# The mixer's input projection by Strassen products, with kept weight sums and equal buffers

## The chip, the cores and the metric

The kernel runs on one core of a Trainium2 chip. The metric is the time of one execution on the device in microseconds. The engines are TensorE (PE: matmuls and transposes; its weight loads, PEld, overlap them), VectorE (DVE), ScalarE (ACT), GpSimd (POOL) and SyncE (SP), on whose queue all DMAs of this kernel are issued. Each engine works through its own instructions in a fixed order and waits on semaphores for the others. SBUF is the memory on the core, PSUM the memory that matmuls write, DRAM lies outside.

## What is computed

One layer of a decoder, for a prompt of 2048 tokens and 32 sample tokens (8 sequences of 4), with a model width of 1024, all in float32. Cut to what matters here:

```python
def token_mixer(xn, mem_k, mem_v, pool_prev, n_prev, lp):       # xn = rmsnorm(x)
    proj = xn @ lp['w_in']                  # 1024 x 4608: u 512 | v 512 | pool 256 | queries 256 | gates 3 x 1024
    u, v = jnp.split(jax.nn.gelu(a_part), 2, axis=-1)
    vn = layernorm(v, lp['gmlp_ln_g'], lp['gmlp_ln_b'])
    br_a = (u * chunk_spatial(vn, ...)) @ lp['w_branch_a']
    br_b = mixed_pools(b_part) @ lp['w_branch_b']               # causal means over 2, 4, 8, 16 tokens
    br_c = cross_attn(q, mem_k, mem_v) @ lp['w_branch_c']       # 4 heads of 64, softmax over 256 memory tokens
    merged = gates[0] * br_a + gates[1] * br_b + gates[2] * br_c
    return merged @ lp['w_out'], vn, new_pool

def decoder_layer(...):
    h = x + rmsnorm(token_mixer(rmsnorm(x), ...))
    out = h + rmsnorm(conv_ffn(rmsnorm(h), ...))                # 1024 -> 2 x 2816 -> 1024
```

## The kernel before

Products that need float32 accuracy are made of three matmuls. Both factors are split into a rounded part (hi) and the rest (lo), and hi x hi, hi x lo and lo x hi are added up in PSUM. `split_unit` (L104) splits a weight tile: ScalarE casts (L109), VectorE subtracts (L110); its results lie in a ring of three buffers, `u`. Weights come into SBUF through the pool `rawp`, two buffers of 8 KB per partition.

The prompt is worked through in four blocks of 512 tokens, 0 to 3; block 1 has the 32 sample tokens too, 544 in all, as two column ranges of 272. For each block `mixer` runs over the columns of `w_in`: the v stage (tokens in rows, `tok_mm`, L129 to L131), then sixteen pairs of 128-column tiles (`mtile`, L124 to L126: 8 steps of depth, three matmuls each, so 24 of 512 columns a tile and 48 a pair): one pair for the pool, one for the queries, two for u and twelve for the gates. Each tile's result is evicted by one ScalarE instruction (L657 for u with its gelu, L695 for a gate with its tanh). After each three gate pairs the three branches' matrices follow for two column tiles (again `mtile`), and VectorE multiplies and adds (L708 to L714).

Between queries and u stands the cross-attention, for four row tiles of 128 tokens: scores (L613), maximum (L619), exponentials (L622), reciprocal and scaling (L624, L626), transposes (L632), their copies to SBUF (L635, one by ScalarE and one by VectorE), the product with the values (L641), and the split of its result (L645, L646). The tiles `pr` (probabilities) and `pT` (transposed) come from the pool `w4` of four buffers of 4 KB, which many short-lived tiles share.

`outproj` multiplies the merged result by `w_out`, normalises and adds x. Beside it, `norm_steps` prepares the next block's x: normalisation (L164), transposes (L174), split (L178, L179). In blocks 2 and 3 `pair_steps` prepares the FFN's x beside the gates: it fetches rows of h from DRAM, scales them (L264), transposes (L275, L277), forms the sums of quarters that Strassen's products need and stores them in DRAM.

The FFN's first matrix is already multiplied by seven Strassen products instead of eight (L873): `right_factors` (L309) forms sums of the weights' quarters (L320 to L324), `blocks` multiplies and combines.

The order of the instructions on each engine is set when the program is built: a scheduler of the framework places each instruction by priority (program order) and by when it takes its operands and buffers to be free. The generators (`next(steps)`) only set where in program order a step stands.

## Time and profile before

| | |
|---|---|
| median of 3 runs | 2811.24 us (2808.88 to 2812.51) |
| the profiled execution | 2814.71 us, span of its instructions 2813.0 us |
| TensorE busy | 2752.8 us, 98% |
| VectorE, ScalarE busy | 1710.2 us (61%), 1037.3 us (37%) |
| mean granted TensorE clock | 0.991 |
| DMA | 337.57 MB, mean 120 GB/s |

The stages in the span: up to 136 us the start, v, pool, queries, attention and u of block 0; to 314 us its gates; to 363 its output projection; block 1 to 760 us with its gates from 504 on; block 2 to 1058; block 3 to 1373; the two halves of the FFN's first matrix to 1845 and 2291; the second matrix to the end. A matmul's end is modelled in these records and successive matmuls overlap; what one costs is the distance between two starts. The granted clock is the share of TensorE's full clock that the chip let through.

### The profile page before, as it was taken

What the parts mean: (1) busy time and instruction counts of PE and PEld (TensorE: products, weight loads), DVE (VectorE), ACT (ScalarE), POOL (GpSimd) and SP (SyncE); (2) the same over time, 40 slices, a digit from 0 to 9 for tenths busy, and PEclk for the clock granted to TensorE, in tenths of its full rate; (3) what the DMA queues carried; (4) which work ended last, traced back from release to release, by engine and by line L of the source; (5) the groups of instructions that cost most, each with busy time, mean ns of one, the idle gap of its engine ahead of it and who ended that gap; (6) DMA issues with size and microseconds to landing.
All of it is one profiled execution on the core that took longest, in us unless ns stands there. A gap on an engine that the chain in (4) does not pass through costs nothing.

```text
span 2813.0 us, 38162 instructions
## 1 busy us (share of the span) xinstructions
PE 2752.8 (98%) x15256; PEld 2361.8 (84%) x15256; DVE 1710.2 (61%) x2777; ACT 1037.3 (37%) x1676; POOL 108.0 (4%) x192
## 2 busy tenths in 40 slices
PE   7999999999999999999999999989999989999998
PEld 6688889999778887888788888889999978888887
DVE  5534465343464546544587877667777756668665
ACT  3532334333554435443554543332332332214112
POOL 1000010000100001000100000000000000001001
PEclk9999999999999999999999999999999999999999
DMA  5323333322325433355553432522122243225322
GB/s 178 113 90 97 125 121 102 102 91 91 125 86 157 155 120 120 113 165 190 206 169 102 141 123 80 204 101 92 61 77 92 69 165 131 90 78 205 109 73 92
DMA packets 256916, 337.57 MB, mean 120 GB/s; under 512 B 16365, under 2 KB 211194, under 8 KB 254938
## 3 DMA queue, kind: packets, MB, share of 16 engines
q1 hardware_dynamic: 256738, 335.13, 35.8%
q8 instruction: 120, 1.97, 0.3%
q14 instruction: 58, 0.48, 0.1%
HBM read 270.22 MB, written 64.96 MB: 119 GB/s over the span
## 4 chain that ended last, share of the span: by engine, by line
issue 52%; PE 42%; DVE 2%; POOL 2%; ACT 1%; DMA 0%; POOLq 0%; SPq 0%; DVEq 0%; ACTq 0%
PE mm L126 10%; PE mm L125 10%; PE mm L124 10%; PE mm L129 2%; PE mm L131 2%; PE mm L130 2%; POOL rs L136 1%; POOL rs L138 1%; PE tp L613 1%; PE tp L641 1%; ACT tp L151 1%; PE mm L439 1%; PE tp L660 1%; PE tp L632 0%; PE tp L174 0%
## 5 line engine op out<-in xcount | busy, mean ns | idle before, releaser
L873 PE MATMUL mm<-X,u 128*128 128x512 f32 (+2 forms) x5544 | 896.5, 323 | 13.4 <-ACT u L109 4.1
L873 PEld LDWEIGHTS mm<-X,u 128*128 128x128 f32 x5544 | 802.9, 190 | 98.5 <-ACT u L109 6.7
L110 DVE TENSOR_TENSOR u<-raw,u 128x1024 fp32r<-128x1024 f32 (+1 forms) x384 | 445.1, 1160 | 514.0 <-ACT u L109 513.7
L109 ACT CAST u<-raw 128x1024 fp32r<-128x1024 f32 (+1 forms) x384 | 382.5, 1000 | 711.4 <-PE mm L131 235.6
L126 PE MATMUL mm<-half,u 128*128 128x512 f32 (+1 forms) x1600 | 566.8, 354 | 4.4 <-DVE u L110 4.4
L124 PE MATMUL mm<-half,u 128*128 128x512 f32 (+1 forms) x1600 | 567.2, 354 | 0.0
L125 PE MATMUL mm<-half,u 128*128 128x512 f32 (+1 forms) x1600 | 566.3, 354 | 0.0
L126 PEld LDWEIGHTS mm<-half,u 128*128 128x128 f32 x1600 | 301.5, 188 | 47.4 <-DVE u L110 5.7
L124 PEld LDWEIGHTS mm<-half,u 128*128 128x128 f32 x1600 | 301.9, 189 | 43.5 <-issue 0.3
L125 PEld LDWEIGHTS mm<-half,u 128*128 128x128 f32 x1600 | 301.7, 189 | 42.3
L1036 DVE TENSOR_TENSOR Y<-Y,mm 128x512 f32<-128x512 f32 (+1 forms) x340 | 212.0, 636 | 135.1 <-PE mm L131 126.4
L129 PE MATMUL mm<-u,a 128*128 128x512 f32 x616 | 242.6, 394 | 7.3 <-ACT a L1023 7.3
L131 PE MATMUL mm<-u,a 128*128 128x512 f32 x616 | 245.6, 399 | 0.4 <-DVE a L1024 0.4
L130 PE MATMUL mm<-u,a 128*128 128x512 f32 x616 | 244.7, 397 | 0.0
L695 ACT ACTIVATE gt<-mm,vb 128x512 f32<-128x512 f32 (+1 forms) x120 | 73.0, 609 | 337.8 <-PE mm L126 337.8
L129 PE MATMUL mm<-u,half 128*128 128x512 f32 (+1 forms) x360 | 145.1, 403 | 2.3 <-ACT half L178 2.3
L129 PEld LDWEIGHTS mm<-u,a 128*128 128x128 f32 x616 | 117.7, 191 | 34.2 <-ACT a L1023 7.5
L131 PE MATMUL mm<-u,half 128*128 128x512 f32 (+1 forms) x360 | 143.0, 398 | 0.0
L130 PE MATMUL mm<-u,half 128*128 128x512 f32 (+1 forms) x360 | 142.6, 396 | 0.0
L130 PEld LDWEIGHTS mm<-u,a 128*128 128x128 f32 x616 | 116.4, 189 | 27.3
L131 PEld LDWEIGHTS mm<-u,a 128*128 128x128 f32 x616 | 116.3, 189 | 27.0 <-DVE a L1024 1.1
L956 DVE SCALAR_TENSOR_TENSOR d<-gE,vecs,d 128x1024 f32<-128x1024 f32 x88 | 112.7, 1280 | 1.2 <-ACT d L954 0.2
(237 smaller groups left out, 2692.7 us busy)
## 6 DMA issues: line engine op xcount, KB each, us to landing
raw<-in_w_in SPq DMA_DIRECT2D x72, 1024.0 KB
raw<-in_w_up SPq DMA_DIRECT2D x44, 1024.0 KB
raw<-in_w_down SPq DMA_DIRECT2D x22, 1024.0 KB
raw<-in_w_out SPq DMA_DIRECT2D x16, 1024.0 KB
act<-d SPq DMA_DIRECT2D x22, 528.0 KB
ar<-act SPq DMA_DIRECT2D x22, 528.0 KB
act<-d SPq DMA_DIRECT2D x22, 512.0 KB
ar<-act SPq DMA_DIRECT2D x22, 512.0 KB
```

Source lines behind the costliest of these rows:

```text
L109: S.copy(uv[:, 0], src)
L110: V.tensor_tensor(uv[:, 1], src, uv[:, 0].bitcast(F32), ALU.subtract)
L124: T.matmul(ps, lhsT=u[:, 0, k], rhs=xk(xT, k, 0, c0, n), start=i == 0, stop=False)
L125: T.matmul(ps, lhsT=u[:, 0, k], rhs=xk(xT, k, 1, c0, n), start=False, stop=False)
L126: T.matmul(ps, lhsT=u[:, 1, k], rhs=xk(xT, k, 0, c0, n), start=False, stop=i == len(ks) - 1)
L129: T.matmul(ps, lhsT=lh, rhs=wh, start=first, stop=False)
L130: T.matmul(ps, lhsT=lh, rhs=wl, start=False, stop=False)
L131: T.matmul(ps, lhsT=ll, rhs=wh, start=False, stop=last)
L695: S.activation(gt[:, c0:c0 + n], ps[:, :n], AF.Tanh, bias=vb[:, i * 8 + j:i * 8 + j + 1], scale=0.5)
L873: T.matmul(ps, lhsT=u[:, wl, k], rhs=x[:, xl, k, c0:c0 + n], start=not more and k + i == 0, stop=k + i == 5, skip_group_check=True)
L956: V.scalar_tensor_tensor(d[j][:, 0:FSB], gE[j][:, k:k + FSB], cw(k, f), d[j][:, 0:FSB], ALU.mult, ALU.add)
L1036: return V.tensor_tensor(yd, yd, ps, ALU.add)
```

## The change

- All sixteen pairs of `w_in` in every block are computed by `blocks`, with the block's tokens in two halves of 256 rows (272 in block 1), the depth in two halves of 512 and the pair's two column tiles as the two halves of the columns: 7 products of 12 matmuls with 256 (272) columns.
- The seven combinations of x are made by `mix_steps` and `pair_steps` in the gate stage of the block before, stored in DRAM (`md`, `m8`, `mf_`) and loaded by `load_block` in the output projection; block 0 makes its own at the start. `norm_steps` and `to_features` are gone.
- The sums of the weights are formed in block 0 by `right_factors` and stored in DRAM (`ws`); blocks 1 to 3 load them by `kept_factors`, 1.75 MB a pair, split as 3.5 tiles of 128x1024.
- A pair's results leave PSUM by one copy (p1) and four instructions of 256 columns on ScalarE and five of 256 columns on VectorE.
- In the v stage the sample rows of block 1 are two parts of 16 rows. The attention over the samples' cached memory now stands directly behind the prompt's attention.
- Buffers: `big`, 6 of 17 KB, becomes 13 of 8.5 KB; `rawp` becomes 4 of 4 KB, `w2` 8 instead of 10; weights and down weights are loaded in smaller pieces. The tile t1 of a pair (p1, v, v7 and one more) is one buffer of `w4`; in the mixer the weight sums `sm` too.

```diff
-    big = ctx.enter_context(tc.tile_pool(name="big", bufs=6))
-    rawp = ctx.enter_context(tc.tile_pool(name="rawp", bufs=2))
+    big = ctx.enter_context(tc.tile_pool(name="big", bufs=13))
+    rawp = ctx.enter_context(tc.tile_pool(name="rawp", bufs=4))
...
+    def mix_steps(b):
+
+        for r1, r2, n, _ in mix_rows(b):
+            for src, i in (r1, r2):
+                xt = w4.tile([P, D], F32, name="xt", tag="w4")
+                DMA.dma_start(xt[:n], src)
+                row_rstd(xt[:n], n, rx[:n, i:i + 1])
+            yield
...
+        yield from pair_steps(items, gx)
...
+    def kept_factors(c):
+
+        return factors_of(split_unit(raw3(load_raw(w_in[:, :, c:c + P]), 8)),
+                          split_unit(raw3(load_raw(ws[c][:, 0:8]), 8)),
+                          split_unit(raw3(load_raw(ws[c][:, 12:16]), 8)[:, 0:4]),
+                          split_unit(raw3(load_raw(ws[c][:, 8:12], w_in[:, 4:8, c + P:c + 2 * P]), 8)))
...
+    def blocks(W, X, c0, n):
+
+
+        if n <= 256:
+            t1 = w4.tile([P, D], F32, name="t1", tag="w4")
+            p1, v, v7, sp = (t1[:, q * 256:q * 256 + n] for q in range(4))
...
+        pa = mm()[:, :n]
+        product(pa, W[1], factor(X, 1), c0, n)
+        S.copy(p1, pa)
+        yield
+        pb = mm()[:, :n]
+        product(pb, W[6], factor(X, 6), c0, n)
+        V.tensor_tensor(v, pb, p1, ALU.subtract)
+        yield
+        product(pa, W[2], factor(X, 2), c0, n, True)
+        yield 0, 0, pa, None, None, sp
+        pc = mm()[:, :n]
+        product(pc, W[7], factor(X, 7), c0, n)
+        V.tensor_tensor(v7, pc, v, ALU.add)
+        yield
+        pe = mm()[:, :n]
+        product(pe, W[4], factor(X, 4), c0, n)
+        yield 1, 0, pe, v7, ALU.subtract, sp
+        pd = mm()[:, :n]
+        product(pd, W[5], factor(X, 5), c0, n)
+        yield 1, 1, pd, v7, ALU.add, sp
+        product(pd, W[3], factor(X, 3), c0, n, True)
+        yield 0, 1, pd, v, ALU.add, sp
...
+            def pair(c):
+                W = kept_factors(c) if b else right_factors(w_in, c)
+                for _, _, (h, *it) in all_blocks(W, X, [(0, w)], False):
+                    yield (h, *it)
...
             for gp in range(2):
-                pu = pair_units(w_in[:, :, gp * 256:gp * 256 + 256])
+                ugs = [w2.tile([P, NTB], F32, name="ug", tag="w2") for _ in range(2)]
+                for h, j, *it in pair(gp * 256):
+                    spread(ugs[j], whole(h, j, *it), h, lambda o, i: S.activation(o, i, AF.Gelu_apprx_tanh))
...
-                    for jj in range(2):
-                        j = 2 * jp + jj
-                        u = pu(jj)
-                        gt = w2.tile([P, NTB], F32, name="gt", tag="w2")
-                        for (c0, n) in subs:
-                            ps = mm()
-                            mtile(ps[:, :n], u, xT, c0, n)
-                            S.activation(gt[:, c0:c0 + n], ps[:, :n], AF.Tanh,
-                                         bias=vb[:, i * 8 + j:i * 8 + j + 1], scale=0.5)
+                    for _ in range(3 if b == 2 else 2):
+                        next(steps, None)
+                    gt = [w2.tile([P, NTB], F32, name="gt", tag="w2") for _ in range(2)]
+                    for h, j, *it in pair(1536 + i * D + jp * 256):
+                        r = i * 8 + 2 * jp + j
+                        spread(gt[j], whole(h, j, *it), h,
+                               lambda o, x: S.activation(o, x, AF.Tanh, bias=vb[:, r:r + 1], scale=0.5))
```

The order of instructions around two places. TensorE in the attention of block 2, before: scores L613, transposes L632, values L641; L124 to L126 are matmuls of the u stage. The excerpt goes from the third row tile's transposes to the fourth's scores.

```order
L126 MATMUL mm<-half,u 128x512
L632 MATMUL tp<-ident,pr 128x128 x6
L124 MATMUL mm<-half,u 128x512
L632 MATMUL tp<-ident,pr 128x128 x2
L641 MATMUL tp<-pT,Vm 64x128 x4
L613 MATMUL tp<-kT,qq 128x256 x4
L641 MATMUL tp<-pT,Vm 64x128 x4
L613 MATMUL tp<-kT,qq 128x256 x8
L125 MATMUL mm<-half,u 128x512
L126 MATMUL mm<-half,u 128x512
L124 MATMUL mm<-half,u 128x512
```

Fifteen matmuls of the u stage stand behind these scores, ahead of the fourth tile's transposes, and about as many ahead of the third's. The same place in the changed kernel, from the second row tile's scores to the third's transposes (scores L719, transposes L738, values L747; L381 are products of the u pair):

```order
L719 MATMUL tp<-kT,qq 128x256 x10
L381 MATMUL mm<-xs,u 128x256 x10
L738 MATMUL tp<-ident,pr 128x128 x8
L747 MATMUL tp<-pT,Vm 64x128 x4
L719 MATMUL tp<-kT,qq 128x256 x2
L747 MATMUL tp<-pT,Vm 64x128 x4
L719 MATMUL tp<-kT,qq 128x256 x10
L738 MATMUL tp<-ident,pr 128x128 x8
```

Ten matmuls of 256 columns stand ahead of the second tile's transposes and none ahead of the third's; the fourth tile is like the third, block 3 like block 2, and in block 0 none stands ahead of any of the four. ScalarE at the end of the same attention in the changed kernel (exponentials L728, copy to pT L741, split of the result L751, the u pair's first copy into t1 L396, its gelu L761):

```order
L728 ACTIVATE pr,sm<-tp,nm 128x256 x4
L741 COPY pT<-tp 128x512
L751 CAST brB<-tp 128x2x128
L728 ACTIVATE pr,sm<-tp,nm 128x256 x4
L741 COPY pT<-tp 128x512
L396 COPY t_8804<-mm 128x256
L751 CAST brB<-tp 128x2x128
L761 ACT_TABLE_LOAD
L761 ACTIVATE ug<-t_8804 128x256
```

The copy of the u pair's first product now stands behind the fourth row tile's exponentials and copy.

## Rows read from the trace of the kernel before

**Rows 1.** The page: busy time and share of the span, by engine.

```profile
span 2813.0 us, 38162 instructions
PE 2752.8 (98%) x15256; PEld 2361.8 (84%) x15256; DVE 1710.2 (61%) x2777; ACT 1037.3 (37%) x1676; POOL 108.0 (4%) x192
```

**Rows 2.** Stages: length, busy us and instructions by engine, clock, DMA share, GB/s.

```profile
0.00:136.00 136.00, 117.66 (x562) 85.51 (x563) 72.98 (x125) 55.46 (x113) 15.00 (x33) 0.96 0.46 150
136.00:314.00 178.00, 178.00 (x770) 143.81 (x769) 74.60 (x85) 56.46 (x76) 6.49 (x7) 1.00 0.28 90
...
504.00:684.00 180.00, 180.00 (x1426) 179.33 (x1426) 72.40 (x109) 57.44 (x91) 0.97 (x3) 1.00 0.28 91
...
760.00:840.00 80.00, 77.80 (x425) 61.10 (x424) 53.39 (x92) 40.16 (x83) 6.72 (x12) 1.00 0.23 73
...
1146.00:1328.00 182.00, 182.00 (x805) 147.47 (x804) 83.10 (x122) 68.97 (x102) 0.10 (x1) 1.00 0.48 152
```

**Rows 3.** The same view of a stretch of 256-column products in the FFN.

```profile
2052.00:2059.00 7.00, 7.00 (x62) 7.00 (x61) 3.36 (x7) 2.75 (x4) 0.00 (x0) 1.00 0.00 0
```

**Rows 4.** Block 2's attention in order of time: start, duration, engine, line, operation.

```profile
797.93 0.98 PE L613 MATMUL tp<-kT,qq 64*128 64x256 f32 x12
...
803.83 1.03 PE L632 MATMUL tp<-ident,pr 128*128 128x128 f32 x8
...
805.10 0.66 PE L641 MATMUL tp<-pT,Vm 128*64 128x128 f32 x8
...
808.01 0.48 ACT L622 ACTIVATE pr<-tp,nm 128x256 f32<-128x256 f32 x1
...
812.54 0.69 DVE L635 COPY pT<-tp 128x512 f32<-128x512 f32 x1 [0.78 <-PE tp L632]
...
814.37 0.97 PE L613 MATMUL tp<-kT,qq 64*128 64x256 f32 x8
815.27 1.29 DVE L619 TENSOR_REDUCE nm<-tp 128x2 f32<-128x512 f32 x2
815.99 0.47 ACT L622 ACTIVATE pr<-tp,nm 128x256 f32<-128x256 f32 x1 [1.13 <-DVE nm L619]
...
818.18 1.14 DVE L626 TENSOR_SCALAR pr<-pr,sm 128x256 f32<-128x256 f32 x4
819.55 0.59 ACT L635 COPY pT<-tp 128x512 f32<-128x512 f32 x1 [0.69 <-PE tp L632]
```

**Rows 5.** Gaps and clock: matmuls in order of time, and stretches as in rows 2.

```profile
47.11 0.80 PE L126 MATMUL mm<-half,u 128*128 128x512 f32 x1 [2.96 <-DVE u L110]
...
1397.47 0.33 PE L275 MATMUL tp<-ident,fx 128*128 128x128 f32 x1 [3.49 <-ACT fx L264]
...
43.00:69.00 26.00, 23.05 (x94) 18.31 (x93) 18.84 (x38) 2.72 (x4) 4.38 (x4) 0.93 0.42 136
...
46.80:50.20 3.40, 3.09 (x7) 2.48 (x8) 2.94 (x6) 0.00 (x0) 2.38 (x3) 0.50 0.18 74
...
1398.50:1401.90 3.40, 3.40 (x11) 2.72 (x10) 3.40 (x8) 2.12 (x4) 0.00 (x0) 0.50 0.55 152
```

**Rows 6.** Instructions by shape: busy us, mean ns of one, idle before and its causes.

```profile
L110 DVE TENSOR_TENSOR u<-raw,u 128x1024 fp32r<-128x1024 f32 x340 | 415.1, 1222 | 513.3 <-ACT u L109 513.1
...
L126 PE MATMUL mm<-half,u 128*128 128x512 f32 x960 | 379.9, 396 | 4.4 <-DVE u L110 4.4
L109 ACT CAST u<-raw 128x1024 fp32r<-128x1024 f32 x340 | 355.2, 1049 | 658.0 <-PE mm L131 235.6 <-PE mm L126 125.2 <-PE mm L873 108.2
...
L695 ACT ACTIVATE gt<-mm,vb 128x512 f32<-128x512 f32 x72 | 49.6, 689 | 230.3 <-PE mm L126 230.3
...
L320 DVE TENSOR_TENSOR sm<-raw 128x512 f32<-128x512 f32 x44 | 30.2, 686 | 5.8 <-DMA raw<-in_w_up 5.5
...
L622 ACT ACTIVATE pr<-tp,nm 128x256 f32<-128x256 f32 x64 | 29.7, 474 | 9.6 <-DVE nm L619 9.5
...
L974 DVE TENSOR_TENSOR d<-d,t 128x256 f32<-128x256 f32 x66 | 27.7, 420 | 0.6
```

More of the change, by code (lines that the diff above doesn't have):

```diff
@@ L268, in pair_steps @@
         yield
-        for e, (s, rows, n, c0, k) in enumerate(items):
+        for e, (rows, n, k, split, sums) in enumerate(items):
             f = nxt
@@ new lines, in split_sums, with load_block @@
+    def split_sums(x):
+        hi, lo = x[:, 0], x[:, 1]
+        S.copy(hi, lo.bitcast(F32))
+        V.tensor_tensor(lo, lo.bitcast(F32), hi.bitcast(F32), ALU.subtract)
+    def load_block(b, own=None):
+        X = own or {"A": []}
+        if own is None:
+            for k in range(4):
+                X["A"].append(hb([P, 2, 4, mw[b]], name="xa"))
+                DMA.dma_start(X["A"][k].bitcast(F32), md[b][:, k])
+            X[8] = hb([P, 2, 4, mw[b]], name="x8")
+            DMA.dma_start(X[8].bitcast(F32), m8[b])
+        for i in (6, 5, 3):
+            X[i] = hb([P, 2, 4, mw[b]], name="xs")
+            DMA.dma_start(X[i][:, 1].bitcast(F32), mf_[b][:, XF.index(i)])
+            split_sums(X[i])
+        return X
@@ new lines, in product @@
+    def product(ps, u, x, c0, n, more=False):
+        for k in range(4):
+            for i, (wl, xl) in enumerate(((0, 0), (0, 1), (1, 0))):
+                T.matmul(ps, lhsT=u[:, wl, k], rhs=x(k, xl)[:, c0:c0 + n], start=not more and k + i == 0,
+                         stop=k + i == 5, skip_group_check=True)
+    def blocks(W, X, c0, n):
+        if n <= 256:
+            t1 = w4.tile([P, D], F32, name="t1", tag="w4")
+            p1, v, v7, sp = (t1[:, q * 256:q * 256 + n] for q in range(4))
+        else:
+            t1 = w4.tile([P, D], F32, name="t1", tag="w4")
+            t2 = w4.tile([P, D], F32, name="t2", tag="w4")
+            p1, v, v7, sp = t1[:, 0:n], t1[:, 512:512 + n], t2[:, 0:n], t2[:, 512:512 + n]
+        pa = mm()[:, :n]
[20 more added lines that the diff above has]
+        yield 0, 1, pd, v, ALU.add, sp
@@ new lines, in all_blocks, with whole @@
+    def all_blocks(W, X, subs, together):
+        gens = [(c0, n, blocks(W, X, c0, n)) for c0, n in subs]
+        if together:
+            for its in zip(*(g for _, _, g in gens)):
+                for (c0, n, _), it in zip(gens, its):
+                    if it:
+                        yield c0, n, it
+        else:
+            for c0, n, g in gens:
+                for it in g:
+                    if it:
+                        yield c0, n, it
+    def whole(h, j, ps, add, op, sp):
+        if add is None:
+            return ps
+        dst = sp if (h, j) == (1, 0) else add
+        V.tensor_tensor(dst, ps, add, op)
+        return dst
@@ L549, in mixer @@
+                for dst, sl, m in parts:
+                    src = ps[:, sl]
+                    if m == 4:
+                        src = src.rearrange("p (b c) -> p b c", c=4)
+                    if add is None:
+                        S.copy(dst, src)
+                    else:
+                        a = add[:, sl]
+                        V.tensor_tensor(dst, src, a if m > 4 else a.rearrange("p (b c) -> p b c", c=4), op)
+            for i in range(2):
+                E = Ep[i]
                 V.tensor_copy(C["hal"][:, i], E[:, TB:TB + PSTATE])
@@ L717, in mixer, with outproj @@
+                next(steps, None)
+            mg = []
+            for m in range(4):
+                mg.append(hb([P, 2, 2, NTB], name="mg"))
+                hi, lo = (mg[m][:, hl, :, 0:n_all] for hl in range(2))
+                src = mf[m // 2][:, 2 * (m % 2):2 * (m % 2) + 2, 0:n_all]
+                S.activation(hi, src, AF.Copy, scale=0.5)
+                V.scalar_tensor_tensor(lo, src, 0.5, hi.bitcast(F32), ALU.mult, ALU.subtract)
             return mg
-        def outproj(b, mg, steps, then=None):
+        def outproj(b, mg, steps=None, then=None):
@@ L727, in outproj @@
+            for t in mixt:
+                G.memset(t[:, 2175:2176], 0.0)
+            for t in mixF:
+                G.memset(t[:, 0, 0:1], 0.0)
+            mixr = [mixt[ti // 2][:, (ti % 2) * D:(ti % 2 + 1) * D] for ti in range(nt)]
+            mixv = [[mixr[ti][:, ch * 512:(ch + 1) * 512] for ti in range(nt)] for ch in range(2)]
+            if steps:
+                steps()
             ss2 = [stat.tile([P, 2], F32, name="sso", tag="sso") for _ in range(nt)]
             for ch in range(2):
[L729 to L731 removed]
```

558 lines of the change are left out of this document (245 added, 313 removed).

## The prediction

> **What bounds the kernel now.** I read the page's busy table first, then the table of stages, then single lines and one stretch in order of time. TensorE is busy 98% of the 2813.0 us span and no other engine more than 61% [rows 1]. In the stages of the mixer, the part that changes, it is the same: the twelve gate pairs of block 0 fill 136 to 314 us with TensorE busy 178.00 of 178.00, the u and gate pairs of block 1 fill 504 to 684 us (180.00 of 180.00), and even the stretch of block 2 with its attention (760 to 840 us) leaves only 2.2 us [rows 2]. Only the first 136 us leave 18 us. So time goes away if TensorE issues less, and comes back wherever it has to wait for something that other engines did beside it until now. What one matmul costs is the step between two, not its own duration (matmuls overlap): 178.00 us for 770 records are 0.231 us for 512 columns, 180.00 us for 1426 are 0.126 us for 272 columns [rows 2]. For 256 columns a stretch of the FFN's Strassen products shows 62 records in 7.00 us; about two of them began before it, since records overlap, so the step is 7.00/60 = 0.117 us [rows 3]. Half the columns cost 0.506 of the step: the 7-for-8 saving is kept almost whole.
>
> **What is removed.** Of TensorE: per block 16 column pairs. In blocks 0, 2 and 3 a pair was 48 matmuls of 512 columns and becomes 7 x 12 = 84 of 256: 48 x 0.231 = 11.1 us against 84 x 0.117 = 9.8 us. Over 16 pairs and three blocks: 3 x (768 x 0.231 - 1344 x 0.117) = 3 x 20.2 = 60.5 us. In block 1 both sides run 272 columns: 16 x (96 - 84) x 0.126 = 24.2 us. The v stage of block 1 takes its sample rows in two parts of 16 instead of one of 32: 24 more matmuls of 512, +5.5 us. Net: -79.2 us. The transposes of x move from the output projection into the gate stage (32 per block in both kernels) and cancel.
>
> **The attention loses its cover.** This is the largest term on the other side. Attention handles four row tiles, each a chain: 12 score matmuls (S), maximum, exponentials, reciprocal and scaling on VectorE and ScalarE, 8 transposes (T), copies, 8 value matmuls (V). In the kernel before, u-stage matmuls stand between S and T (the orders above). In the changed kernel the u pair stops there: its partial results need t1 from the pool of four buffers that also holds the attention's pr and pT, and the copy of p1 stands on ScalarE behind the fourth tile's exponentials and copy. Until it is made, the PSUM tiles of the pair are not released. So nothing lies between S and T for all four tiles in block 0 and for two tiles in each other block; for one more tile there 10 matmuls do (1.2 us of some 4).
> What an uncovered tile costs comes from the stretch 797 to 822 us [rows 4]: the last score matmuls end at 814.37 + 0.97 = 815.34; maximum from 815.27, exponentials from 815.99, reciprocal, the four scalings 818.18 to 819.32. The first transposes can start when one pair of heads is scaled, about 818.5 to 818.6: 3.2 us idle. After them the copies of 0.59 and 0.69 us stand before the value matmuls, of which some 0.8 us isn't covered. Idle is thus about 4.0 us a tile, beside TensorE's own 0.98 + 1.03 + 0.66 = 2.7 us. Bounds: 3.2 (copies covered) and 5.3 us (the period of 8.0 us between two tiles' exponentials in that stretch less 2.7); I take 4.0, since in that stretch filling work and splits lie in between, which lengthen it. Count: 4 + 3 x 2.7 = 12.1 tiles, 48.4 us (39 to 64).
>
> **The clock.** These are 13 gaps of 2 to 3.3 us. In this trace a gap of 2.96 us ends at 47.11 us, and from 46.80 to 50.20 us the granted clock is 0.50; another of 3.49 us ends at 1397.47, and from 1398.50 to 1401.90 us the clock is 0.50 again [rows 5]. That is the lower level, 1.2 instead of 2.4 GHz, for 3.4 us each time. Of a tile's period of 6.7 us TensorE works 2.7; if half of a period runs at half speed, about 1.3 us of work take 1.3 us longer. 13 x 1.3 = 16.9 us. Bounds: 0 (the clock stays up) and 13 x 2.7 = 35 us (all of it at the low level).
> The Trainium skill ("TensorE: Matmul & The Clock Gate", section "HAM oscillation - how this bites in real kernels") describes a kernel with short bursts of matmuls between waits in which the clock falls at every wait, so that each burst pays anew. The two stretches of [rows 5] agree with it for single gaps; no stretch of this trace has gaps in a row. By that rule applied to every gap the term would be the upper bound, 35 us, and the sum 18 us higher.
>
> **Block 0 before its gates: VectorE.** Block 0 makes the sums of the weights. Per pair VectorE now does three subtractions of 1.222 us, one of 0.685, four sums of 0.685 and five results of 0.420: 9.2 us instead of 2 x 1.222 = 2.4 [rows 6]. The pool and query pairs of block 0 ran from 43 to 69 us beside 18.84 us of VectorE [rows 5]; they get 13.6 us of this and three more splits of x (3.7 us) on top, so that VectorE has some 36 us where TensorE has 2 x 9.8 = 20. The memory's keys and values follow on VectorE's queue too and hide nothing. Of the 16 us I take 8 as late; part falls beside the v stage, where VectorE is now free of the normalisation's steps. Bounds 0 and 14.
>
> **Block 0's gates.** Per pair TensorE has 9.8 us plus two thirds of a branch unit (24 x 0.231 x 2/3 = 3.7), 13.5 us. VectorE has 9.2, the gate products 2 x 0.685 (taken as any 512 columns), their sums 4/3 x 0.685 and the branch split 2/3 x 1.222 [rows 6], 12.3 us, and per step of the next block's x four differences of 128 columns and a split of 640, an estimate of 1.9 us by the rows for 256, 512 and 1024 columns, for two of three pairs: 13.6 us in all. Two engines equally loaded, in fixed orders, can't both be full: I take 0.5 us a pair, 6 us (0 to 12).
>
> **Blocks 1 to 3: the ring.** A pair needs four split tiles instead of two from a ring of three buffers. The tightest is the last: its buffer comes free after the third product and it is wanted by the sixth, 2 x 12 x 0.117 = 2.8 us later; cast and subtraction take 1.05 + 1.22 = 2.27 us [rows 6]. It fits by half a microsecond when both engines are free, and not when a step for x or for the FFN (on ScalarE four scalings and copies of about 0.5 us and a cast) stands in front. About 32 such steps and 48 pairs: I take 10 us, 0.2 us a pair (0, always hidden, to 25, 0.5 us a pair).
>
> **What costs nothing.** Loads rise from 1 MB to 1.75 MB a pair, and x makes a trip through DRAM. The gate stages before had 90 to 152 GB/s [rows 2] with TensorE full, and 1.75 MB in 13.5 us are 130 GB/s; x and, in block 0, the sums' stores come on top. ScalarE rises from 2 x 1.049 + 2 x 0.689 = 3.5 us a pair to 3.5 x 1.049 + 5 x 0.47 = 6.0 and stays below half of 13.5 [rows 6]. The casts of the merged result at the mixer's end lie beside the first products of the output projection. FFN and down projection change only in buffers. If the loads aren't hidden, it shows as waits for raw tiles.
>
> **Sum.** -79.2 + 48.4 + 16.9 + 8 + 6 + 10 = +10 us on the profiled execution's own 2814.71 us, 2825 us. That execution is 3.5 us above the median of the runs, 2811.24 us, so the forecast is 2821 us.
>
> **Rivals.**
> 1. *The saving stands, the waits are small.* Gaps of 3.2 us a tile (39 us), clock up, splits hidden: -79 + 39 + 0 to 30 for the rest gives 2771 to 2801 us. For it: the splits do fit in the ring by the bare sum, and VectorE is busy only 74.60 of 178 us in block 0's gates now [rows 2]. Against it: the gap of 3.2 us is a chain of dependent instructions, which nothing shortens.
> 2. *The split decides, not TensorE* (clearly slower). If a last split tile is late by 0.8 us in each of 48 pairs, because casts queue on ScalarE behind results that wait for PSUM, that is 38 us instead of 10, and with VectorE 12 us late in block 0's gates the sum is +10 + 28 + 6 = +44, 2855 us. It decides from about 0.5 us a pair. For it: where gate matmuls wait at all now, it is for this subtraction (4.4 us in all) [rows 6]. Against it: the first three tiles of a pair have over 4 us.
> 3. *Every uncovered tile wholly at the low clock:* its 2.7 us take 5.4, 35 instead of 17 us, 2839 us. For it: after both gaps of [rows 5] the clock fell. Against it: it was back at 1.00 after 3.4 us, half of a tile's period.
> The rule of the Trainium skill named above ("TensorE: Matmul & The Clock Gate", the section on oscillation) is what this third case would look like.
> 4. *It doesn't do what it says:* a step for 256 columns in the mixer that is longer than in the FFN, say 0.126 us as for 272, takes back 3 x 1344 x 0.009 = 36 us, 2857 us. Against it: same weights, same loads of weights, and x read from tiles of the same kind. Hardly likely.
>
> **How the numbers follow.** Chances: the forecast, 2806 to 2834 us, 0.42; rival 1 0.31; rival 2 0.14; rival 3 0.10; rival 4 0.03. What a measurement of this kernel can tell from no change is about 0.2%, 5.6 us, so no change is 2806 to 2817: of the forecast's 0.42 some 0.16 lie there, 0.22 above it, and 0.04 of its tail below; of rivals 2 to 4 nearly all is slower. Faster 0.35, same 0.17, slower 0.48. The range 2775 to 2862 us reaches down into rival 1 and up over rivals 2 and 3.
>
> **What would show it.** Gate stages of blocks 1 to 3 shorter by 15 to 20 us each with TensorE near full: the saving is right. In the attention of each block, idle of about 3 us in front of the transposes, ended by the scaling on VectorE, and granted clock between 0.5 and 1 there: the second and third terms are right; if the idle is under 2 us or the clock stays at 1.00, they are too large. Waits of the products for the subtraction of a split beyond 25 us in all: rival 2. Idle in the first 136 us not above 18: the term for block 0 is wrong. The prediction as a whole fails if TensorE's idle grows by less than 30 us or by more than 130.

## The result, and the profile after

The changed kernel takes 2916.55 us (median of 4 runs, 2912.26 to 2918.28) against 2811.36 us of the kernel before: a ratio of 1.0373, 95% interval [1.0355, 1.0391]. It is 105 us slower. The forecast was 2821 us, with a range up to 2862 us: the sign was right, the size wrong by a factor of ten. The page's busy table of the kernel after, to be read beside [rows 1]:

```profile
span 2910.5 us, 44323 instructions
...
PE 2747.3 (94%) x16833; PEld 2430.1 (83%) x16833; DVE 2009.8 (69%) x3438; ACT 1246.7 (43%) x2144; POOL 109.4 (4%) x201
```

TensorE is busy as long as before (2752.8 us), although the forecast took 79 us of matmuls from it: it idles 163 us instead of 60, and the mean granted clock fell from 0.991 to 0.971. If p of the span is granted 0.5, the mean is 1 - p/2, so by this estimate the time at the lower of the two levels went from 51 to 169 us.

Where it lies shows in the starts of the matmuls, cut into stages by their lines (us). Two of the experiments below stand beside (e1, and e16 as the last version); what they change is told there.

| stage | before | after | pr, pT moved | last version |
|---|---|---|---|---|
| start to the end of v, block 0 | 40 | 39 | 40 | 41 |
| to the first scores, blocks 0, 1, 2, 3 | 56, 33, 27, 25 | 61, 31, 29, 27 | 60, 32, 30, 29 | 66, 32, 32, 28 |
| attention and u, blocks 0, 2, 3 | 40, 42, 42 | 57, 57, 56 | 40, 44, 44 | 44, 44, 45 |
| gates, blocks 0, 2, 3 | 178, 182, 182 | 208, 204, 173 | 213, 209, 177 | 186, 181, 171 |
| block 1: attention, samples, u, gates | 255 | 271 | 273 | 273 |
| output projection and next v | 76, 80, 69, 44 | 78, 76, 66, 45 | 78, 76, 66, 44 | 78, 75, 66, 44 |
| FFN up, FFN down | 927, 505 | 918, 505 | 918, 505 | 922, 506 |

The same as stages of the kernel after (columns as in [rows 2]): attention of block 0, pool and queries of block 1, attention of block 2, then the gates of blocks 0, 2 and 3.

```profile
100.00:137.00 37.00, 23.48 (x155) 18.13 (x156) 17.33 (x41) 13.55 (x43) 0.00 (x0) 0.68 0.08 24
443.00:473.00 30.00, 26.05 (x187) 23.94 (x186) 28.87 (x68) 12.85 (x27) 5.51 (x7) 1.00 0.29 92
...
850.00:890.00 40.00, 30.65 (x216) 24.69 (x215) 23.23 (x50) 16.71 (x48) 0.00 (x0) 0.76 0.20 60
...
157.00:365.00 208.00, 186.20 (x1261) 172.29 (x1260) 160.18 (x273) 114.24 (x206) 8.29 (x14) 0.93 0.67 206
...
907.00:1111.00 204.00, 183.80 (x1264) 167.57 (x1263) 140.49 (x245) 121.06 (x214) 4.72 (x10) 0.97 0.76 234
1260.00:1433.00 173.00, 170.82 (x1234) 160.52 (x1234) 124.44 (x203) 97.19 (x158) 0.20 (x2) 1.00 0.68 213
```

In the attention TensorE is busy for 23.48 of 37 us at clock 0.68. In the gates of blocks 0 and 2 it idles 20 us each and the clock is below 1; block 3, with half of block 2's steps and no weight sums, has neither and is 9 us faster than before. So 46 us were lost in three attentions, 52 in two gate stages, 16 in block 1.

The attention went as its order said. TensorE in block 1 of the kernel after, in order of time:

```profile
491.60 0.98 PE L719 MATMUL tp<-kT,qq 64*128 64x256 f32 x10
495.91 1.94 PE L738 MATMUL tp<-ident,pr 128*128 128x128 f32 x8 [3.34 <-DVE pr L732]
497.78 1.13 PE L747 MATMUL tp<-pT,Vm 128*64 128x128 f32 x8
498.84 0.79 PE L719 MATMUL tp<-kT,qq 64*128 64x256 f32 x2
499.56 1.13 PE L747 MATMUL tp<-pT,Vm 128*64 128x128 f32 x8
500.62 1.65 PE L719 MATMUL tp<-kT,qq 64*128 64x256 f32 x10
```

Between scores and transposes 3.34 us pass until the scaling on VectorE, and after the gap the eight transposes take 1.94 us instead of 1.03 and the value matmuls 1.13 instead of 0.66 [rows 4]: half clock.

The gates are another matter. A gate stage has four equal quarters, each of three pairs and two column tiles of the branches. Their lengths (us), and how far into the stage the transposes of the steps reach that prepare the next x or the FFN's x:

| gates | after | steps until | last version | steps until |
|---|---|---|---|---|
| block 0 | 52, 69, 45, 42 | 122 | 45, 54, 45, 42 | 109 |
| block 1 | 51, 52, 45, 45 | 72 | 48, 49, 45, 45 | 70 |
| block 2 | 54, 67, 41.5, 41.5 | 99 | 43, 49, 47, 41.5 | 125 |
| block 3 | 47.5, 43, 41.5, 41.5 | 48 | 43, 45, 41.5, 41.5 | 54 |

Where no step is left, a quarter takes 42 us (45 in block 1, with its samples), in block 0 too, whose last quarter forms and stores weight sums like the others. The loss lies in the quarters with steps. The two halves of block 2's gates in the kernel after:

```profile
907.00:1009.00 102.00, 84.32 (x589) 75.37 (x588) 70.51 (x145) 71.79 (x144) 4.53 (x8) 0.97 0.88 265
1009.00:1111.00 102.00, 99.49 (x678) 92.20 (x677) 69.98 (x101) 49.27 (x70) 0.20 (x2) 0.98 0.64 203
```

What a step does there shows in order of time. First SyncE's queue, then TensorE, in block 2's gates of the kernel after (start, duration of the issue):

```profile
978.28 0.56 SPq L262 DMA_DIRECT2D md<-xh  x1
978.90 0.56 SPq L264 DMA_DIRECT2D m<-xh  x1
979.56 0.41 SPq L262 DMA_DIRECT2D md<-fx  x1
980.02 0.57 SPq L264 DMA_DIRECT2D m<-fx  x1
980.68 1.20 SPq L241 DMA_DIRECT2D fx<-in_x_prompt  x2
981.93 1.23 SPq L100 DMA_DIRECT2D raw<-ws  x1
983.27 0.56 SPq L254 DMA_DIRECT2D mf<-fx  x1
983.88 0.62 SPq L100 DMA_DIRECT2D raw<-in_w_in  x1
984.66 0.50 SPq L262 DMA_DIRECT2D md<-xh  x1
```

```profile
985.10 0.84 PE L227 MATMUL tp<-ident,fx 128*128 128x128 f32 x4 [1.61 <-ACT fx L243]
989.22 0.80 PE L381 MATMUL mm<-xs,u 128*128 128x256 f32 x2 [3.29 <-ACT u L114]
990.48 2.50 PE L381 MATMUL mm<-xs,u 128*128 128x256 f32 x10 [0.46 <-DVE u L115]
```

A step of x (one quarter of the depth for 128 row pairs) issues seven DMAs, a step of the FFN's x five. The seven are two fetches, one store of the sums and four of the split combinations, each 0.4 to 0.6 us of the queue, some 3.8 us in all, in one order with the raw tiles. Here the raw tile is issued at 983.88, lands, is cast, and TensorE, which had waited for the step's rows at the head of its own order just before, waits 3.29 us for the cast; the next ten matmuls of 256 columns take 2.50 us, about twice the usual.

In block 0's gates the longest waits are others: TensorE's for the copy of p1, and ScalarE's, with that copy, for a tile of w4 (total us, times, longest).

```profile
PE mm L381 <- ACT t L396: 12.4, 4, 4.8
ACT t L396 <- DMA m<-fx: 7.1, 3, 3.8
```

There t1 stands behind a step's tile until that tile's store has landed.

### The profile page after: what moved, and what is told of

It reads as the page before. It is cut to its first block, busy times and chain, and to the rows that moved or that the text cites. A ratio compares the mean times of both kernels' runs of the same rounds, so it can differ in the third digit from the quotient of the medians.

```text
span 2910.5 us, 44323 instructions
## 1 busy us (share of the span) xinstructions
PE 2747.3 (94%) x16833; PEld 2430.1 (83%) x16833; DVE 2009.8 (69%) x3438; ACT 1246.7 (43%) x2144; POOL 109.4 (4%) x201
## 4 chain that ended last, share of the span: by engine, by line
issue 48%; PE 7%; POOL 1%; ACT 1%; DVE 1%; DMA 0%; POOLq 0%; SPq 0%; DVEq 0%; ACTq 0%
PE mm L381 4%; POOL rs L137 1%; PE mm L126 1%; PE mm L127 1%; PE mm L125 1%; PE mm L130 0%; PE mm L132 0%; PE mm L131 0%; DMA fx<-hd 0%; POOL rs L139 0%; PE tp L747 0%; ACT pr L728 0%; PE tp L738 0%; ACT mix L852 0%; ACT tp L152 0%
## 5 line engine op out<-in xcount | busy, mean ns | idle before, releaser
L381 PE MATMUL mm<-X,u 128*128 128x512 f32 (+2 forms) x5544 | 893.0, 322 | 7.7 <-ACT u L114 2.6
L381 PEld LDWEIGHTS mm<-X,u 128*128 128x128 f32 x5544 | 799.9, 189 | 91.5 <-ACT t L396 3.9
L114 ACT CAST u<-raw 128x1024 fp32r<-128x1024 f32 (+1 forms) x496 | 471.6, 956 | 832.8 <-PE mm L132 356.4
L115 DVE TENSOR_TENSOR u<-raw,u 128x1024 fp32r<-128x1024 f32 (+1 forms) x496 | 546.8, 1104 | 257.7 <-ACT u L114 249.3
L381 PE MATMUL mm<-xa,u 128*128 128x256 f32 (+1 forms) x3072 | 434.4, 293 | 30.4 <-ACT t L396 17.4
L381 PEld LDWEIGHTS mm<-xa,u 128*128 128x128 f32 x3072 | 400.3, 195 | 44.3 <-ACT t L396 22.4
L381 PE MATMUL mm<-xs,u 128*128 128x256 f32 (+1 forms) x2304 | 337.2, 294 | 27.7 <-ACT u L114 18.2
L381 PEld LDWEIGHTS mm<-xs,u 128*128 128x128 f32 x2304 | 304.9, 196 | 41.8 <-ACT u L114 21.7
L1104 DVE TENSOR_TENSOR Y<-Y,mm 128x512 f32<-128x512 f32 x268 | 183.3, 686 | 126.5 <-PE mm L132 126.1
L435 DVE TENSOR_TENSOR t<-mm,t 128x256 f32<-128x256 f32 (+2 forms) x279 | 127.2, 456 | 82.9 <-PE mm L381 81.0
L396 ACT COPY t<-mm 128x256 f32<-128x256 f32 (+2 forms) x130 | 52.8, 406 | 163.9 <-PE mm L381 151.0
L400 DVE TENSOR_TENSOR t<-mm,t 128x256 f32<-128x256 f32 (+2 forms) x130 | 61.2, 471 | 52.0 <-PE mm L381 47.5
L795 ACT ACTIVATE gt<-t,vb 128x256 f32<-128x256 f32 (+1 forms) x180 | 79.7, 464 | 38.5 <-DVE t L435 38.0
L130 PE MATMUL mm<-u,mg 128*128 128x512 f32 x224 | 88.5, 396 | 0.6 <-ACT mix L854 0.6
```

What stands on the lines that cost most here:

```text
L114: S.copy(uv[:, 0], src)
L115: V.tensor_tensor(uv[:, 1], src, uv[:, 0].bitcast(F32), ALU.subtract)
L130: T.matmul(ps, lhsT=lh, rhs=wh, start=first, stop=False)
L381: T.matmul(ps, lhsT=u[:, wl, k], rhs=x(k, xl)[:, c0:c0 + n], start=not more and k + i == 0, stop=k + i == 5, skip_group_check=True)
L400: V.tensor_tensor(v, pb, p1, ALU.subtract)
L435: V.tensor_tensor(dst, ps, add, op)
```

## The experiments

"The moved version" is the first one. What each measured is a median of a few runs; the kernel before took 2811 to 2816 us beside each of them, so that a difference of 5 us between two experiments decides nothing.

**pr and pT elsewhere** (e1).

```diff
-                pr = w4.tile([P, 4, M], F32, name="pr", tag="w4")
+                prt = hb([P, 2176], F32, name="prt")
+                pr, pT = (prt[:, q * D:(q + 1) * D] for q in range(2))
...
-                pT = w4.tile([P, 4, 2, P], F32, name="pT", tag="w4")
```

> The changed kernel, but each row tile's pr and pT lie in one of the 13 large buffers instead of two of the four w4 buffers, so that the u pair's t1 no longer waits for them; u-stage products stand between scores and transposes again. Theory A (the lost cover of the attention, with the low clock that follows, is about two thirds of the loss): the stretch from the first scores to the end of the u stage goes from some 57 us back to 40 to 42 us in blocks 0, 2 and 3, granted clock 1.00 there, the gate stages of blocks 0 and 2 stay at 208 and 204 us, total 2845 to 2860 us. Rival B (the chain itself, not the order, sets the attention's length): under 15 us gained in all, about 2905 us.

2889.9 us, 27 us gained, between the two expectations. For the attention theory A is right, for the gates and the total it isn't: attention of block 0 and of block 2, then the gates of blocks 0 and 2:

```profile
100.00:137.00 37.00, 35.40 (x314) 31.61 (x312) 29.78 (x60) 26.73 (x59) 0.00 (x0) 1.00 0.56 178
...
843.00:887.00 44.00, 42.29 (x367) 38.33 (x368) 34.80 (x70) 32.34 (x70) 0.00 (x0) 1.00 0.41 127
...
141.00:354.00 213.00, 186.80 (x1240) 172.62 (x1239) 161.85 (x275) 115.70 (x211) 9.39 (x14) 0.91 0.65 200
...
887.00:1096.00 209.00, 185.93 (x1253) 170.63 (x1252) 140.77 (x246) 122.65 (x218) 4.90 (x10) 0.93 0.74 223
```

17, 13 and 12 us less in blocks 0, 2 and 3, at clock 1.00. Block 1 keeps its gaps (clock 0.72 from 463 to 500 us); why was not tested. The gates of blocks 0 and 2 then take 5 us longer each, those of blocks 1 and 3 take 1 and 3, and the stages ahead of the attention in blocks 1 to 3 take 1 to 2: part of the gain is given back at once.

**t1 in a pool of its own, with three raw buffers** (e2), **and three raw buffers alone** (e3).

```diff
-    rawp = ctx.enter_context(tc.tile_pool(name="rawp", bufs=4))
+    rawp = ctx.enter_context(tc.tile_pool(name="rawp", bufs=3))
...
-            t1 = w4.tile([P, D], F32, name="t1", tag="w4")
+            p1 = upool["t1"].tile([P, 272], F32, name="p1", tag="p1")[:, 0:n]
+            t3 = upool["t1"].tile([P, 3 * 272], F32, name="t3", tag="t3")
```

> The changed kernel, but p1 and v, v7, sp of a pair lie in a pool of their own (paid for by three instead of four raw buffers); pr and pT stay in w4. Theory C (in the gate stages of blocks 0 and 2 the pair waits for a w4 buffer that a step's tile holds until its store to DRAM has landed): attention as in the run before, and on top the gate stages go from 208 and 204 us to 185 or less, total 2800 to 2825 us. Rival D (there the transfers themselves are late, DMA share 0.67 and 0.76): gate stages stay above 198 us, total as in the run with pr and pT moved, 2845 to 2860 us.

> The changed kernel with three instead of four raw buffers and nothing else: the price of what the run with t1's own pool pays. Theories A and C: within 8 us of 2916.5 us. Rival D: raw tiles come later still, 15 us or more slower, most of it in the gate stages of blocks 0 and 2.

2940.2 and 2960.7 us. One raw buffer fewer costs 44 us, so the price spoils the comparison with 2916.5; against its own control t1's pool gains 20 us, most of it in the attention of blocks 2 and 3 (45 and 44 us against 57 and 56: its order has the cover back), and nothing in the gates (220 and 217 us against 221 and 213). Theory C, as put here, falls; raw tiles in time matter.

**Filler in the gaps** (e4): thrown-away matmuls, everything else as in the changed kernel.

```diff
+                    for _ in range(26 if hp == 0 else 0):
+                        T.matmul(t[:, 0:M], lhsT=kT[:, 0, 0, 0:P], rhs=kT[:, 0, 0], start=True, stop=True)
```

> The changed kernel with 26 matmuls of 256 columns (3.0 us) whose result is thrown away in front of each row tile's transposes, 16 times: the same chain, but TensorE is kept busy in the gap. If the granted clock's fall costs what I think (measured period of an uncovered tile 8.1 to 9.7 us, 6.6 us at full clock): idle in front of the transposes under 0.6 us, clock 1.00 in the attention, period 6.5 to 7 us, total 15 to 35 us faster than 2916.5 us although 48 us of useless work are added. If the period is set by the chain alone: no period shorter than 8 us, total the same or up to 12 us slower (three or four tiles that had cover).

2917.2 us, no change. The attention of block 0, and the gates behind it:

```profile
101.00:133.00 32.00, 31.21 (x271) 26.05 (x270) 17.72 (x42) 14.68 (x44) 0.00 (x0) 1.00 0.11 34
152.00:361.00 209.00, 187.57 (x1263) 173.89 (x1262) 159.49 (x273) 113.97 (x206) 8.43 (x14) 0.93 0.67 205
```

The clock stays at 1.00 and the stage from the first scores to the end of u is shorter by 6, 3, 4 and 3 us in blocks 0 to 3, 17 us with all the useless work in it. At least that is what the low clock cost there, since the filler also lengthens the few tiles that had cover; it is about the size of my term (16.9). But the time did not fall by the 15 to 35 us expected: the gates of blocks 1 to 3 grew by 3, 8 and 3 us and the stages ahead of the attention by a little too. A stage that is paced by something else takes back what is gained ahead of it.

**The steps' DMAs on GpSimd's queue** (e5), on the moved version.

```diff
-                DMA.dma_start(part, src.rearrange("p (h k c) -> p h k c", h=2, k=4)[:, :, k])
+                G.dma_start(part, src.rearrange("p (h k c) -> p h k c", h=2, k=4)[:, :, k])
```

> The run with pr and pT in a large buffer (2889.9 us), and the DMAs of the steps (fetch and stores of x's and h's combinations) and the stores of the weight sums issued on GpSimd's queue instead of SyncE's; same bytes, same buffers. Theory E (SyncE's queue works in order at 0.4 to 0.6 us an issue and waits in order for the steps' results, so raw loads behind them come late): gate stages from 213, 193, 209 and 177 us to 185 or less in blocks 0 and 2 and 175 to 180 in block 1 and 172 in block 3, total 2820 to 2840 us. Rival D (bandwidth: same bytes): gate stages within 6 us of what they were, total 2880 to 2895 us. Rival F (VectorE and ScalarE loads): the same as D.

2959.0 us, 69 slower, outside every expectation. GpSimd is busy 397.5 us instead of 109, and its queue carried 76 MB. What TensorE waited for (total us, times, longest), in the moved version and in this one:

```profile
PE tp L227 <- ACT fx L243: 21.0, 14, 3.3
```

```profile
PE tp L227 <- ACT fx L243: 61.2, 38, 4.9
```

The steps' transposes come up at the head of TensorE's order before their rows are there, 38 times instead of 14. Whatever the order on SyncE's queue costs, the other queue cost more, so the run decides nothing between E and D; but it shows that a late step stops TensorE itself.

**One more small issue ahead of each raw tile** (e6), on the moved version; 440 DMAs of 8 KB in all.

```diff
+        junks.append(hdp.tile([P, 16], F32, name=f"junk{len(junks)}"))
+        DMA.dma_start(junks[-1], x2[0:P, 0:16])
```

> The run with pr and pT in a large buffer, and one more DMA on SyncE's queue ahead of each raw tile, of 8 KB from DRAM to DRAM into a tile of its own that nobody reads: the issue cost once more, hardly any bytes. Theory E: some 0.4 us x 3.5 to 5 a pair more in a queue that is late already: gate stages of blocks 0 and 2 10 to 30 us longer each, total 2915 to 2960 us. Rival D or F: under 5 us slower in all.

2905.8 us, 16 slower, with 3 us each in the gates of blocks 0 to 2: less than theory E wanted, more than its rivals. The issue time counts, but it is not the whole.

**Sums formed anew in each block** (e7), on the moved version.

```diff
-                W = kept_factors(c) if b else right_factors(w_in, c)
+                W = right_factors(w_in, c)
```

> The run with pr and pT in a large buffer, and the weight sums formed anew in every block instead of kept in DRAM: no stores of sums in block 0, 2 raw loads of 0.5 MB a pair instead of five issues of 1.75 MB in blocks 1 to 3, but four more VectorE sums (2.7 us) a pair there. Theory E: block 0's gates 10 to 20 us shorter; blocks 1 to 3 between 10 us shorter and 5 us longer each; total 2850 to 2885 us. Rival D: shorter by more, 2850 us or less, since the bytes fall by 43%. Rival F (VectorE's load decides): blocks 1 to 3 longer by 15 us or more each, total 2920 us or more.

2977.4 us, 88 slower: gates of block 1 from 193 to 221, block 2 from 209 to 226, block 3 from 177 to 189 us, and block 0 unchanged (215) although it stores no sums. Fewer bytes didn't help; 2.7 us of VectorE a pair (and a tile for the sums in w4) hurt, about as theory F, VectorE's load, expected (2920 us or more). They hurt beside the steps: the last quarter of block 2's gates stays at 42 us, its first goes from 61 to 75. The run doesn't tell VectorE's time from the tile in w4. Rival D, bandwidth, is out as the first cause, and keeping the sums is the right half of the change.

**More buffers**, on the moved version: w4 of five (e8), t1 apart besides (e9), and rows fetched two steps ahead (e10); six raw buffers (e11). The room comes from reloading three gain rows a block.

```diff
-    w4 = ctx.enter_context(tc.tile_pool(name="w4", bufs=4))
+    w4 = ctx.enter_context(tc.tile_pool(name="w4", bufs=5))
...
+        upool["raw"] = m2ctx.enter_context(tc.tile_pool(name="rawm", bufs=2, reuse_waits="tile"))
```

> The run with pr and pT in a large buffer (2889.9 us), and w4 with five buffers instead of four; the room comes from reloading the layer norm's gain and offset and the post-norm's gain in each block instead of keeping them, and the FFN's spare step buffer is the fifth of w4. Theory C2 (in the gate stages a pair's t1, the weight sums and three tiles of a step share four buffers, each held until its store has landed; ScalarE and TensorE wait for them in order, and each gap takes the clock down): block 0's gates from 213 to 195 to 203 us, block 2's from 209 to 195 to 203, total 2860 to 2875 us. Rivals D (bandwidth) and E (SyncE's order): gates within 5 us, total 2885 to 2897 us.

> As the run with five w4 buffers, and t1 (p1 and v, v7, sp) in a pool of its own besides, with all four raw buffers. Theory C2: the waits of the products for the copy of p1 (12.3 us in block 0's gates, 2.6 and 3.2 in blocks 1 and 2) and half of the low clock go; gates 185 to 195 us in blocks 0 and 2, total 2835 to 2860 us. Rivals D and E: within 8 us of the run before.

> As the run with t1 in its own pool and five w4 buffers, and each step's rows are fetched two steps ahead instead of one. Theory C2: TensorE's waits in front of the steps' transposes (3.9 and 10.4 us in the gates of blocks 0 and 2) go, with 5 to 10 us of low clock: 10 to 20 us faster than that run. Rival E: the fetches only stand elsewhere in SyncE's queue, within 5 us. Rival G (another tile in w4 takes away what the own pool gave): slower by 5 to 15 us.

> The run with pr and pT in a large buffer (2889.9 us), and six raw buffers instead of four during the mixer, paid for by reloading the layer norm's gain and offset and the post-norm's gain in each block; w4 stays at four buffers with t1 in it. Theory R (a raw tile is now half as large and a pair needs 1.75 MB instead of 1, so four of them reach only some 11 us ahead instead of 22; loads stand on SyncE's queue behind the steps' DMAs that wait for results, and come late): the gates of blocks 0 and 2 go from 213 and 209 us to 190 to 198, of block 1 from 193 to 185, total 2840 to 2865 us. Rival E alone (the queue's order, whatever the buffers) or D (bandwidth): within 8 us of 2890.

2886.0, 2891.6, 2889.5 and 2888.4 us: nothing, though single gate stages moved (block 0's from 213 to 204, 200 and 196 us with the first three, block 2's from 209 to 200 with raw tiles); block 1's attention and u took 2 to 6 us more. As accounts of the total, theories C2 and R fall: four raw buffers are just enough in this order, and buffers alone do not pay, although block 0's gates do wait for w4.

**Steps late, fewer stores** (e12): a step stands behind the products of a pair instead of ahead of its loads, and x8 is stored with the other combinations, five DMAs a step instead of seven; six raw buffers. **The same with five raw buffers and t1 apart** (e13).

```diff
-                    for _ in range(3 if b == 2 else 2):
-                        next(steps, None)
...
+                    for n_, (h, j, *it) in enumerate(pair(1536 + i * D + jp * 256)):
+                        if n_ < (3 if b == 2 else 2):
+                            next(steps, None)
...
-                DMA.dma_start(split[0][hl], src[:, 0:4 * n].rearrange("p (i c) -> p i c", i=4))
-                if len(split) > 1:
-                    DMA.dma_start(split[1][hl], src[:, 4 * n:5 * n])
+                DMA.dma_start(split[0][hl], src[:, 0:m].rearrange("p (i c) -> p i c", c=n))
```

> As the run with six raw buffers, and the steps of x and h stand behind the products of a gate pair in program order instead of ahead of the pair's loads, and the fifth combination of x (x8) is stored together with the four others: two DMAs fewer of seven a step. Theory E (SyncE's order): 10 to 30 us faster than the run with six raw buffers, gates of blocks 0 and 2 under 190 us. Theory R alone: within 6 us of it.

> As the run before (steps late, fewer stores), but five raw buffers and t1 in a pool of its own instead of six raw buffers. If with raw tiles in time the pair's wait for t1 in w4 comes to light (theory C2 behind R): 5 to 20 us faster than that run. If raw buffers count for more: 5 to 25 us slower.

2870.7 us, 18 less than with six raw buffers alone, and 2861.6 us, 9 less again. Block 0's gates came down from 214 to 195 and then 187 us, block 1's from 198 to 192 and 185; block 2's stayed at 198 and 202 (200 with six raw buffers alone). The order of steps and loads, with the two stores fewer, is a cause (the runs do not part the two), and only behind it does t1's own buffer pay in the total. What holds block 2, by the waits of TensorE in its gates in the second of these runs (total us, times, longest; the lines of this kernel are four or five further on):

```profile
PE tp L231 <- ACT fx L247: 11.9, 9, 4.2
PE mm L382 <- DVE u L120: 3.1, 4, 1.2
```

The steps' transposes, in TensorE's order, wait for rows that were fetched late.

**Rows fetched two steps ahead** (e14), **and two steps a pair in block 2 instead of three** (e15); **the latter with rows one step ahead** (e16).

```diff
-                        if n_ < (3 if b == 2 else 2):
+                        if n_ < 2:
```

> As the run with late steps, five raw buffers and t1 apart (2861.6 us), and in the mixer each step's rows are fetched two steps ahead. There the steps' transposes, which stand in TensorE's order, wait 11.9 us (9 times) in block 2's gates and 4.2 us in block 0's for rows that are still to be fetched and scaled. Theory H (late fetches at the head of TensorE's queue, each with low clock after it): block 2's gates from 203 to 185 to 192 us, total 10 to 22 us faster. Rival I (the fetch takes its place in SyncE's queue and DMA from raw tiles): within 5 us, the waits only change their cause.

> As the run before, and block 2 makes two steps a gate pair like the other blocks instead of three; what is left over comes beside its output projection. Theory H and E (three steps a pair are too many for the queues of SyncE, ScalarE and VectorE in order): block 2's gates 175 to 185 us, its output projection up to 8 us longer, total 5 to 15 us faster. If the steps' density doesn't matter: within 4 us, or slower by what the output projection loses.

> The run with late steps, fewer stores, five raw buffers and t1 apart (2861.6 us), with two steps a gate pair in block 2 instead of three and rows fetched one step ahead as at first. The density of the steps cost 17 us in block 2's gates in the last run; nothing else moves: block 2's gates 183 to 188 us, blocks 0 and 1 at 185 to 192, total 2840 to 2850 us. If the gain hung on the fetch two steps ahead: 2855 to 2862 us.

2877.9, 2857.0 and 2837.6 us. Fetching earlier makes it 16 us slower: rival I, and worse. Fewer steps a pair do it: block 2's gates fall from 202 to 185 and 181 us. No step is left for its output projection, which stays at 66 us; that some would be was a wrong expectation. The gate stage has room for all of them, and their transposes now reach to 125 us of it instead of 106. Its third quarter, which had none, goes from 41.5 to 47 us, the second from 69 to 49. The last version's gates of block 2 and TensorE's longest wait in them:

```profile
870.00:1051.00 181.00, 175.09 (x1252) 163.64 (x1251) 140.57 (x248) 118.63 (x216) 3.65 (x10) 0.99 0.84 258
```

```profile
PE tp L231 <- ACT fx L247: 4.4, 4, 2.3
```

The clock is 0.99 there. More bytes a second (258 GB/s, DMA share 0.84) pass than in the changed kernel's 204 us: bandwidth wasn't the limit. This is the best version: ratio 1.0091 [1.0076, 1.0106] to the kernel before, still slower.

**The pool's sums on GpSimd** (e17), beside the last.

```diff
-                V.tensor_tensor(s[:, :, 13:L], E[:, :, 13:L], E[:, :, 12:L - 1], ALU.add)
+                G.tensor_tensor(s[:, :, 13:L], E[:, :, 13:L], E[:, :, 12:L - 1], ALU.add)
```

> As the run beside it, and the running sums of the pool's windows (six VectorE additions of some 0.3 to 0.7 us a block, more for the samples) are made by GpSimd. Between the v stage and the attention VectorE is busy 29.9 of 32 us in block 1, so theory F (VectorE is the bound there, with 6.45 us a pair where it had 2.4) expects 2 to 4 us less in each block, 8 to 15 us in all. Rival: GpSimd's additions are so much slower, or slow VectorE so much, that the pooled products come later: 0 to 15 us slower.

2852.2 us, 15 slower, as the rival said: an addition of 512 columns takes GpSimd 1.0 to 2.0 us (VectorE 0.69), and the stage grew by 1 to 4 us in each block. It doesn't show whether VectorE bounds the stage. For that speaks only the row above: 28.87 us of VectorE in 30 us of block 1, and the same stretch of the kernel before had 26.59 in 34:

```profile
390.00:424.00 34.00, 31.77 (x227) 30.00 (x227) 26.59 (x60) 10.88 (x23) 5.70 (x8) 0.95 0.25 80
```

## Why the prediction was wrong

1. **The saving** was sized too large. A pure stretch of the gates after, in block 3:

```profile
1352.00:1362.00 10.00, 10.00 (x85) 10.00 (x84) 1.00 0.37 109
```

Less the two records that began before it, 10.00/83 = 0.120 us a matmul of 256 columns, not the 0.117 of the FFN [rows 3]. That is rival 4's mechanism at a third of its size: 3 x 1344 x 0.003 = 12 us of the 79. The saving itself is there: a quarter of the gates without steps takes 41.5 us, where the gates before took 178 to 182 us, 44.5 to 45.5 a quarter.

2. **The attention** was right in place, mechanism and about in size. Idle ahead of the transposes of an uncovered tile 3.2 to 3.5 us (forecast 3.2), clock 0.68 to 0.81; all its waits for the scaling are 39.4 us and for the copies 1.5, 41 us where 48.4 were forecast, since the copies hardly made TensorE wait; the stages grew by 17, 15 and 14 us in blocks 0, 2 and 3 where the sum of saving, idle and clock gave 19, 12 and 12. The clock's share, 17 us or somewhat more, is what the filler took away. The step from there to the total was too simple: 42 us came back in the stages and 27 in the time.

3. **Block 0 before its gates:** first scores at 99.9 instead of 96.2 us, +4 where 8 less 2.5 was expected. The longest wait of the products there, 5.0 us, is for a cast that waits for VectorE's sum of weights. Right.

4. **The step that failed** is "What costs nothing", and with it the two small terms beside it, "Block 0's gates" (6 us) and "the ring" (10 us). I weighed the moved steps by their bytes and by each engine's mean load. With the saving less a few us of transposes they gave gates of some 175 us for blocks 0 and 2; measured are 208 and 204, about 60 us more in two stages, with long single waits that take the clock down with them. All of it lies in the quarters with steps. VectorE's load in block 0's gates, which my term priced, costs nothing where no step is left, and the ring neither: those quarters take 42 us, the pace of the products and branches alone (3 x 84 x 0.120 + 48 x 0.231 = 41.3). What a step brings, as the waits in the traces read, is in the order of four engines at once; what each of them costs was not parted: seven issues on SyncE between raw tiles, scalings on ScalarE that wait for the fetch with the casts of weights behind them, transposes on TensorE that wait for the scaling with products behind them, tiles of w4 that wait for a store. Shown are: the order (steps behind the loads, and two stores fewer: 18 us), the density (two steps a pair instead of three: 21 us of block 2's gates, 24 in all), t1 once the others are relieved (9 us). Not the bytes (e7, e16), and not the number of buffers alone (e8 to e11).

5. **Rival 2** came nearest: slower through splits that come late. But its mechanism, ScalarE behind results that wait for PSUM, isn't what was measured, and its sign did not come: the products waited 15.3 us in all for subtractions of a split, not beyond 25 (for casts 24.9). Its price of 0.8 us a pair was far too small for waits of 3 to 5 us.

6. **The range** ended at 2862 us because every term had its upper end at what one engine's load could do, and none at a queue in which several wait for each other. The sign for the whole did not catch it either: TensorE's idle grew by 103 us, inside the 30 to 130 named, while the time left the range, since the sign counts idle time alone and not work at the lower clock.

What stays open: how the steps' loss in the gates divides between the orders of SyncE, ScalarE, TensorE and VectorE and the tiles of w4, since each experiment moved more than one of them (the small issues alone cost 16 us); what thinner steps would give in blocks 0 and 1, where no version tried them; the 15 to 18 us of block 1, where no version had the cover back; and whether VectorE bounds the pool and query stage. With all that was found the change still loses 0.9%.

## What to carry to other kernels

Work that is moved into a full stage has to be counted in queue places, not in bytes or busy time: list, for every in-order queue, what stands behind each of its instructions that waits. Where the tightest queue can't be found by giving it buffers, thin out the moved work (fewer steps a pair; here the second half of the stage stood empty), and put it behind the loads in program order. Before a product is made cheaper, look at what it covers: a chain of dependent work that ran beside it costs its whole length once the cover is gone, and more while the clock is down.

## What the runs showed of the hardware

The issue of one of a step's DMAs held SyncE's queue for 0.39 to 0.60 us (medians by kind in the kernel after; single ones took up to 1.6): 440 more issues, of 8 KB each, cost 16 us. The steps' transfers and the stores of the weight sums, 76 MB, on GpSimd's queue made that engine busy for 287 us more and the kernel 69 us slower. After ten gaps of 3.2 to 3.5 us on TensorE the eight transposes behind them ran at granted clock 0.50 nine times (1.94 us instead of 1.03) and once partly so (1.31 us); 26 thrown-away matmuls in each gap kept the clock of the attention at 1.00 and made the stage shorter, not longer.
